# Chunk scores in two matmuls of 128 rows, squares of the FFN's norm summed on VectorE, first weights in quarters

## Chip, cores and metric

The kernel runs on one core of one Trainium2 chip. The metric is the time of one execution on the device in microseconds; the median of three runs is given, and one further execution was profiled. Data are in float32; TensorE multiplies in fp32r, so each operand is held as a high half and the rest.

## The reference

Two layers, each an attention block with three groups of heads and a gated FFN with a causal convolution, for 512 positions of width 1024. The part that the change touches:

```python
def chunk_attention(h, rel_bias):
    q, k, v = [t.reshape(B, nc, CHUNK, CH_HEADS, CH_HD) for t in jnp.split(h, 3, axis=-1)]
    ...
    s = jnp.einsum('bnqhd,bnkhd->bnhqk', q, kb).astype(jnp.float32) * (CH_HD ** -0.5)
    ...
    p = jax.nn.softmax(s, axis=-1)
...
for l in range(DEPTH):
    proj = rms_norm(x, attn_norm[l]) @ w_in[l]
    h_mla, h_diff, h_ch = jnp.split(proj, [IN_MLA, IN_MLA + IN_DIFF], axis=-1)
    ...
    x = x + jnp.concatenate([o_mla, o_diff, o_ch], axis=-1) @ w_out[l]
    x = x + conv_ffn(rms_norm(x, ffn_norm[l]), w_ffn_in[l], ffn_conv_w[l], ffn_conv_b[l], w_ffn_out[l])
```

There are 4 chunk heads of 64 dimensions, 6 MLA heads and 6 differential heads. `rms_norm` divides by the root of the mean of squares over the 1024 columns.

## The kernel before

Positions lie along the free axis: x is held transposed as 8 tiles of 128 x 512 in `xa`, and a product (`proj`) takes 128 columns of weights in 24 matmuls of 512 columns: for 8 tiles of x, high weights with the high and the rest of x, then the rest of the weights with the high of x. Weights arrive by SP into one of two raw slots (`wraw`), are split into `wh` and `wl`, and pass through rings of three. PSUM has three banks for products (psproj), two for scores (pss), two for transposes and norms (pspt), one for values (psav).

The jobs of a layer stand in a queue (`ORDER`): kv, q0, q1 and so on for the latent part, d0 to d2 (query and key of two differential heads each), c0 and c1 (query and key of two chunk heads each), values, then the output projection a0 to a7 (inputs that are ready early) and b0, b1 (the last two inputs, four tiles of x each). A job starts when its gate opens. Beside the queue two streams run: `scores`, which takes the heads in the order m, d, c (`HEADS`), two heads of each name, four row blocks each, and `products`, which turns and multiplies the probabilities. A planner (`Clock`) keeps a model of costs, lets the first ready step go to PE, and at the end lists all instructions of all engines in a new order by a critical path (`list_schedule`). All instructions are issued from there, so the profile shows nearly all of them under one line, L364, and groups are told apart by tiles: `af` holds float32 scratch, `ar` the split operands and probabilities.

- A chunk score (`chunk_head`, `three`) multiplies 64 rows: high with high, high with rest, rest with high, three matmuls a row block. The two heads of a tile use rows 0 to 63 and 64 to 127. A differential score has its operands stacked to 96 rows by copies on POOL's queue (`stack`), an MLA score has 128 rows.
- The FFN's norm (`Gain.add`) splits each tile of x after the output projection has been added to it (`add_to_x`, VectorE): ScalarE makes the high half, VectorE the rest, ScalarE the square, and POOL adds the square to the sum (`gain_f.add(..., pool)` in `run_b`). `add_to_x` also frees the product's bank.
- At the start `load_inputs` issues x tile by tile, with the first product's weights in two halves before and after the first tile, the second product's (also two halves) behind the second tile; the third product's follow when a raw slot is free. PE also sums the squares of x itself (`Gain.squares`, pspt from `af` and `ones`).

Of the kernel before, what the change touches and what calls it, by code (L numbers as in the profile page):

```python
# [20 lines left out]
S = 512  # L21
# [31 lines left out]
for u in range(2):  # L53
    RINGS_R[f"cq{u}"], RINGS_R[f"ck{u}"] = ([RINGS_R["kmla"][2 * u + n]] for n in range(2))
    RINGS_R[f"vc{u}"] = [v[1 + u]]
# [8 lines left out]
p0, o0, ol0 = (RINGS_F[t][1] for t in ("P", "o", "ol"))  # L64
RINGS_F["oc"], RINGS_F["om"], RINGS_F["od"] = (S, o0[0:2]), (S, o0[0:3]), (S, o0[3:6])
# [15 lines left out]
ORDER = "kv q0 q1 kr e0 v e1 u0 u1 u2 d0 d1 d2 e2 c0 c1 g0 g1 a0 a1 a2 a3 a4 a5 a6 a7 b0 b1"  # L81
# [8 lines left out]
AHEAD = 1  # L90
NB_OUT = 1 << (8 // KB).bit_length() - 1
# [388 lines left out]
def encoder(ctx, tc, xT, pos_row, pos_col, wflat, small, lam, relx, cst, out):  # L480
# [17 lines left out]
    def T(tag):  # L498
        turn[tag] = turn.get(tag, -1) + 1
        if tag in RINGS_R:  # L500
            n = RINGS_R[tag][turn[tag] % len(RINGS_R[tag])]
            return ar[:, n * 1024 : (n + 1) * 1024]
        w, starts = RINGS_F[tag]
        o = starts[turn[tag] % len(starts)]
        return af[:, o : o + w]
# [33 lines left out]
    def weights(l, name, run, finish, gate=lambda: True):  # L539
        o, c = offs[l, name]  # L540
        runs = [(0, c // 2), (c // 2, c)] if l == 0 and len(work.jobs) < 3 else [(0, c)]
# [4 lines left out]
        def fetch():  # L546
            raw = T("wraw")
            part(raw, *runs[0])
            if work.jobs[0].raw is None:
                rest_of_first.append(lambda: part(raw, *runs[1]))  # L550
            elif len(runs) > 1:
                part(raw, *runs[1])
            return raw
# [35 lines left out]


# [19 lines left out]
    def load_inputs():  # L610

        work.jobs[0].fetch()
        sp.dma_start(sm[0], small[0])
        for k in range(KD):
            sp.dma_start(xs[k], xT[:, k, :])
            if k == 0:
                rest_of_first.pop()()
            if k == 1:
                work.jobs[1].fetch()
        sp.dma_start(posk_i, bass.AP(tensor=pos_row.tensor, offset=0, ap=[[0, P], [1, S]]))  # L620
        sp.dma_start(ct, cst)
        sp.dma_start(posq_i, pos_col)
# [260 lines left out]
    def layer(l, gain_a):  # L883
# [52 lines left out]
        def chunk_qk(u):  # L936
            gate = lambda: (1, 1, 1) in stacks if u else ("m", 2, 1) in scored
            return [qk_unit(f"cq_{u}", f"cq{u}", gate, imm=CH_SCALE), qk_unit(f"ck_{u}", f"ck{u}", gate)]
# [130 lines left out]
        def chunk_head(h, qt, kt, buf, res):  # L1069
            rbias = biases[h]  # L1070
            yield from softmax_rows(three(qt, kt, 64 * (h % 2), 64), lambda i: rbias[:, S - 128 * (i + 1) :], -1.0, res, buf)
            scaled(*res)
            if h + 2 < CH_H:
                biases.append(load_bias(h + 2))
# [69 lines left out]
        def run_b(t, w):  # L1144
            for n in range(NB_OUT):
                c = slice(128 * KB * n, 128 * KB * (n + 1))
                acc = yield from proj(og[KA:], (w[0][:, c], w[1][:, c]), [])
                add_to_x(NB_OUT * t + n, acc)
                gain_f.add(NB_OUT * t + n, pool)

        jobs = {}

        def job(name):
            kind, t = name[0], int(name[1:]) if name[1:].isdigit() else 0
            return {
                "c": lambda: chunk_qk(t),
# [94 lines left out]
        if l == 0:  # L1251
            load_inputs()
            exp_tables()
            work.jobs[0].load()
            for k in range(KD):
                gain_a.split(k)
                if k in (1, 4):
                    work.jobs[1 + k // 4].load()
            gain_a.squares()
            setup_rope()  # L1260
# [9 lines left out]
        def scores():  # L1270
            for n, (kind, u, j) in enumerate(heads):

                over = max((k + 1 for k in range(n) if bufs[k] in bufs[n] + "X" * (kind == "d")), default=0)
                need = [jobs[f"u{u}"]] if kind == "m" else jobs[f"{kind}{u}"][:2]
# [252 lines left out]
```

## Time and profile before

| what | value |
|---|---|
| median of three runs | 1240.6 us (1240.38 to 1242.81) |
| the profiled execution | 1241.23 us, its span 1239.1 us |
| PE busy | 1215.1 us, 5607 matmuls |
| VectorE (DVE), ScalarE (ACT), POOL busy | 861.0, 704.2, 123.0 us |
| mean granted clock of TensorE | 0.995 |

An engine's busy time is the union of its instructions. A matmul's row shows its start and its duration with the latency of the pipeline, so rows of PE overlap; the cost of one in a stream is read from ends. In brackets behind a row stands the idle time before it, with what ended it.

### The profile page before, as it was taken

What the parts mean: (1) busy time and instruction counts of PE and PEld (TensorE: products, weight loads), DVE (VectorE), ACT (ScalarE), POOL (GpSimd) and SP (SyncE); (2) the same over time, 40 slices, a digit from 0 to 9 for tenths busy, and PEclk for the clock granted to TensorE, in tenths of its full rate; (3) what the DMA queues carried; (4) which work ended last, traced back from release to release, by engine and by line L of the source; (5) the groups of instructions that cost most, each with busy time, mean ns of one, the idle gap of its engine ahead of it and who ended that gap; (6) DMA issues with size and microseconds to landing.
All of it is one profiled execution on the core that took longest, in us unless ns stands there. A gap on an engine that the chain in (4) does not pass through costs nothing.

```text
span 1239.1 us, 15626 instructions
## 1 busy us (share of the span) xinstructions
PE 1215.1 (98%) x5607; PEld 991.1 (80%) x5607; DVE 861.0 (69%) x1596; ACT 704.2 (57%) x1233; POOL 123.0 (10%) x181
## 2 busy tenths in 40 slices
PE   8999999999999999999999999999999999999996
PEld 5788887788888888888877888777888888888885
DVE  7798997588774357665457889976876633677643
ACT  6797996765443234444477899876544422444432
POOL 0214310130000000000011143003100000000000
PEclk9999999999999999999999999999999999999998
DMA  5848961733322332323477498436333233332232
GB/s 169 188 104 186 227 134 43 166 103 122 102 87 82 104 105 100 102 81 91 127 163 163 100 235 175 93 79 151 103 102 102 77 97 116 102 96 91 79 97 79
DMA packets 51613, 146.33 MB, mean 118 GB/s; under 512 B 6480, under 2 KB 9552, under 8 KB 51536
## 3 DMA queue, kind: packets, MB, share of 16 engines
q1 hardware_dynamic: 37280, 106.27, 28.1%
q0 software_dynamic: 14256, 39.07, 17.5%
q8 instruction: 44, 0.72, 0.2%
q14 instruction: 33, 0.27, 0.1%
HBM read 132.21 MB, written 2.10 MB: 108 GB/s over the span
## 4 chain that ended last, share of the span: by engine, by line
PE 92%; DVE 3%; ACT 2%; DMA 2%; issue 1%; SPq 0%; DVEq 0%; ACTq 0%; POOLq 0%
PE psproj L364 80%; PE pss L364 5%; PE pspt L364 4%; PE psav L364 3%; DVE af L364 1%; DVE ar L364 1%; DMA ar<-in_wflat 1%; ACT ar L364 1%; ACT af L364 1%; DVE xa L364 1%; DMA xa<-in_xT 1%; DMA af<-in_wflat 0%; SPq L364 0%; ACT L880 0%; ACT rope L364 0%
## 5 line engine op out<-in xcount | busy, mean ns | idle before, releaser
L364 PE MATMUL psproj<-ar 128*128 128x512 f32 (+1 forms) x4595 | 1104.7, 392 | 8.3 <-DVE xa L364 2.2
L364 PEld LDWEIGHTS psproj<-ar 128*128 128x128 f32 x4595 | 849.3, 188 | 184.7 <-DVE ar L364 4.7
L364 ACT CAST ar<-af 128x512 fp32r<-128x512 f32 (+4 forms) x333 | 268.4, 820 | 219.8 <-PE psproj L364 195.7
L364 DVE TENSOR_TENSOR ar<-af,ar 128x512 fp32r<-128x512 f32 (+4 forms) x260 | 239.7, 925 | 145.3 <-PE psproj L364 79.3
L364 DVE SCALAR_TENSOR_TENSOR af<-af,sma 128x511 f32<-128x511 f32 (+1 forms) x192 | 141.9, 748 | 7.5 <-ACT af L364 4.9
L364 ACT ACTIVATE af<-af,sma 128x512 f32<-128x512 f32 x88 | 71.3, 816 | 121.2 <-DVE af L364 121.2
L364 DVE TENSOR_TENSOR af<-psproj,af 128x512 f32<-128x512 f32 x108 | 73.6, 686 | 61.4 <-PE psproj L364 61.0
L364 POOL DMA_DIRECT2D ar<-in_wflat x61 | 54.0, 886 | 617.8 <-ACT ar L364 601.0
L364 ACT ACTIVATE af<-af 128x512 f32<-128x512 f32 (+1 forms) x106 | 65.4, 622 | 71.6 <-DVE af L364 71.0
L364 ACT ACTIVATE af<-af,mn 128x128 f32<-128x128 f32 (+3 forms) x176 | 98.2, 559 | 7.4 <-DVE mn L364 7.0
L364 PE MATMUL pss<-ar 128*128 128x128 f32 (+7 forms) x336 | 88.1, 333 | 0.6 <-DVE mn L364 0.4
L364 PEld LDWEIGHTS pss<-ar 128*128 128x128 f32 (+2 forms) x336 | 56.6, 187 | 19.4 <-issue 7.7
L364 DVE TENSOR_TENSOR xa<-xa,psproj 128x512 f32<-128x512 f32 (+1 forms) x65 | 43.5, 674 | 40.4 <-PE psproj L364 40.3
L364 DVE TENSOR_TENSOR af<-af 128x512 f32<-128x512 f32 (+2 forms) x71 | 48.0, 677 | 33.4 <-ACT af L364 33.0
L364 DVE TENSOR_TENSOR ar<-pspt,ar 128x512 fp32r<-128x512 f32 (+1 forms) x106 | 63.2, 603 | 6.3 <-ACT ar L364 3.5
L364 PE MATMUL psav<-ar 128*128 128x512 f32 (+3 forms) x256 | 64.9, 331 | 0.3 <-DVE af L364 0.2
L364 PE MATMUL pspt<-ident,af 128*128 128x128 f32 x360 | 63.3, 275 | 0.3 <-DVE af L364 0.3
L364 ACT ACTIVATE ar<-af 128x1024 fp32r<-128x1024 f32 (+3 forms) x61 | 58.0, 950 | 8.0 <-PE psproj L364 5.6
L364 PEld LDWEIGHTS pspt<-ident,af 128*128 128x128 f32 x360 | 45.2, 140 | 14.4 <-DVE af L364 2.3
L364 PEld LDWEIGHTS psav<-ar 128*128 128x128 f32 x256 | 44.6, 189 | 8.8 <-issue 1.3
L364 ACT CAST ar<-pspt 128x512 fp32r<-128x512 f32 (+1 forms) x73 | 37.6, 524 | 17.1 <-PE pspt L364 15.5
L364 DVE CUSTOM_DVE_ANT_0 af<-pss,dist 128x384 f32<-128x384 f32 (+2 forms) x96 | 45.3, 484 | 2.9 <-PE pss L364 2.8
(67 smaller groups left out, 564.2 us busy)
## 6 DMA issues: line engine op xcount, KB each, us to landing
af<-in_wflat SPq DMA_DIRECT2D x125, 512.0 KB, 3.5
ar<-in_wflat POOLq DMA_DIRECT2D x37, 512.0 KB, 8.0
af<-in_wflat SPq DMA_DIRECT2D x48, 384.0 KB, 3.0
af<-in_wflat SPq DMA_DIRECT2D x38, 320.0 KB, 2.9
ar<-ar POOLq DMA_DIRECT2D x72, 128.0 KB, 6.2
ar<-in_wflat POOLq DMA_DIRECT2D x16, 384.0 KB, 6.2
xa<-in_xT SPq DMA_DIRECT2D x8, 256.0 KB, 6.8
af<-in_wflat SPq DMA_DIRECT2D x8, 256.0 KB, 3.8
```

Source lines behind the costliest of these rows:

```text
L364: self.clock.issue(self.name, op, outs, ins + aps, func, lambda: fn(*args, **kw))
```

## The change

Chunk scores: `chunk_qk` becomes `chunk_q` and `chunk_k`. A query tile now holds, for each of its two heads, the high half in the head's own 64 rows and the rest in the other 64. A key tile for each head holds high and rest in its own rows, and a copy on POOL's queue puts the same into the other 64 rows. Two matmuls of 128 rows then sum all four products. The keys of the second head of each pair need another slot (`cy`, the first two slots of ring x, which the stacks of the last differential heads read from), so the gate of both key jobs is the last stack of the differential heads. The key jobs have their own names, y0 and y1, in the queue: c0 y0 c1 y1.

FFN's norm: `gain_f.add` is called without POOL, so the squares are summed on VectorE.

Start: the first three products' weights come in four quarters each, one of each product with every second tile of x, and the third product has a raw slot of its own (`wfirst`).

```diff
...
+    RINGS_R[f"cy{u}"] = [RINGS_R["x"][u]]
...
+RINGS_F["wfirst"] = (2 * S, o0[0:1])
...
-ORDER = "kv q0 q1 kr e0 v e1 u0 u1 u2 d0 d1 d2 e2 c0 c1 g0 g1 a0 a1 a2 a3 a4 a5 a6 a7 b0 b1"
+ORDER = "kv q0 q1 kr e0 v e1 u0 u1 u2 d0 d1 d2 e2 c0 y0 c1 y1 g0 g1 a0 a1 a2 a3 a4 a5 a6 a7 b0 b1"
...
+FIRST = 4
...
-        runs = [(0, c // 2), (c // 2, c)] if l == 0 and len(work.jobs) < 3 else [(0, c)]
+        first = l == 0 and len(work.jobs) < 3
+        step = c // FIRST if first else c
+        runs = [(a, a + step) for a in range(0, c, step)]
+        ring = "wfirst" if first and len(work.jobs) == 2 else "wraw"
-            raw = T("wraw")
-            part(raw, *runs[0])
-            if work.jobs[0].raw is None:
-                rest_of_first.append(lambda: part(raw, *runs[1]))
-            elif len(runs) > 1:
-                part(raw, *runs[1])
+            raw = T(ring)
+            if first:
+                rest_of_first.append([lambda a=a, b=b: part(raw, a, b) for a, b in runs])
+            else:
+                part(raw, 0, c)
...
+    def high(src, hi):
+        n = hi.ap[-1][1]
+        if clock.through("act", 0.1 + n / 1200, src) < clock.through("dve", 0.07 + n / 1920, src) + LATE["hs"]:
+            act.copy(hi, src)
+        else:
+            dve.tensor_copy(hi, src)
...
-        work.jobs[0].fetch()
+        for n in range(3):
+            work.jobs[n].fetch()
-            if k == 0:
-                rest_of_first.pop()()
-            if k == 1:
-                work.jobs[1].fetch()
+            if k % (KD // FIRST) == 0:
+                for parts in rest_of_first:
+                    parts.pop(0)()
...
-        def chunk_qk(u):
-            gate = lambda: (1, 1, 1) in stacks if u else ("m", 2, 1) in scored
-            return [qk_unit(f"cq_{u}", f"cq{u}", gate, imm=CH_SCALE), qk_unit(f"ck_{u}", f"ck{u}", gate)]
+        def chunk_q(u):
+            def finish(job, acc, rb):
+                f = tmp("ev")
+                dve.scalar_tensor_tensor(f, acc, CH_SCALE, rb, op0=ALU.mult, op1=ALU.mult)
+                t = pair(f"cq{u}")
+                for j in range(2):
+                    own, other = slice(64 * j, 64 * j + 64), slice(64 - 64 * j, 128 - 64 * j)
+                    high(f[own, :], t[own, j, :])
+                    dve.tensor_tensor(t[other, j, :], f[own, :], t[own, j, :].bitcast(F32), op=ALU.subtract)
+                job.set(t)
+            return unit(f"cq_{u}", gain_a, finish, lambda: (1, 1, 1) in stacks if u else ("m", 2, 1) in scored)
+        def chunk_k(u):
+            def finish(job, acc, rb):
+                f = tmp("ev")
+                dve.tensor_tensor(f, acc, rb, op=ALU.mult)
+                ks = [pair(f"ck{u}"), pair(f"cy{u}")]
+                for j, t in enumerate(ks):
+                    own, other = slice(64 * j, 64 * j + 64), slice(64 - 64 * j, 128 - 64 * j)
+                    high(f[own, :], t[own, 0, :])
+                    dve.tensor_tensor(t[own, 1, :], f[own, :], t[own, 0, :].bitcast(F32), op=ALU.subtract)
+                    pool.dma_start(t[other, :, :], t[own, :, :])
+                job.set(ks)
+            return unit(f"ck_{u}", gain_a, finish, lambda: (2, 1, 1) in stacks)
...
-            yield from softmax_rows(three(qt, kt, 64 * (h % 2), 64), lambda i: rbias[:, S - 128 * (i + 1) :], -1.0, res, buf)
+            yield from softmax_rows([(qt[:, h % 2, :], kt[h % 2][:, n, :]) for n in range(2)], lambda i: rbias[:, S - 128 * (i + 1) :], -1.0, res, buf)
...
-                gain_f.add(NB_OUT * t + n, pool)
+                gain_f.add(NB_OUT * t + n)
-                "c": lambda: chunk_qk(t),
+                "c": lambda: chunk_q(t),
+                "y": lambda: chunk_k(t),
...
-            work.jobs[0].load()
+            for n in range(3):
+                work.jobs[n].load()
-                if k in (1, 4):
-                    work.jobs[1 + k // 4].load()
...
-                need = [jobs[f"u{u}"]] if kind == "m" else jobs[f"{kind}{u}"][:2]
+                need = [jobs[f"u{u}"]] if kind == "m" else jobs[f"d{u}"][:2] if kind == "d" else [jobs[f"c{u}"], jobs[f"y{u}"]]
...
```

What the planner makes of it, in three places. On PE, in layer 0's chunk heads, before (pss are scores, psproj products, psav values, pspt transposes; 128 is what a score writes, the rows that it reads are not printed):

```order
L364 MATMUL psproj_63<-ar 128x512 x4
L364 MATMUL psproj_65<-ar 128x512
L364 MATMUL psproj_63<-ar 128x512
L364 MATMUL pss_67<-ar 128x512 x3
L364 MATMUL psav_70<-ar 128x512
L364 MATMUL psproj_63<-ar 128x512
L364 MATMUL psproj_65<-ar 128x512
L364 MATMUL pspt_69<-ident,af 128x128 x2
L364 MATMUL psproj_65<-ar 128x512
```

and now, at the first chunk head of layer 0:

```order
L368 MATMUL psproj_63<-ar 128x512
L368 MATMUL pss_67<-ar 128x256 x2
L368 MATMUL psproj_63<-ar 128x512
L368 MATMUL psproj_65<-ar 128x512 x2
L368 MATMUL psproj_63<-ar 128x512 x3
L368 MATMUL psav_70<-ar 128x512
L368 MATMUL pss_66<-ar 128x384 x2
L368 MATMUL psproj_64<-ar 128x512
L368 MATMUL pspt_69<-ident,af 128x128 x2
```

A row block's scores were three and are two; what stands between them is of the same kinds.

On VectorE, in the norm of layer 1's FFN, before (xa are additions to x, which free a product's bank; SCALAR_TENSOR_TENSOR from xa are the splits):

```order
L364 TENSOR_TENSOR xa<-xa,psproj_63 128x512
L364 SCALAR_TENSOR_TENSOR ar<-xa,sma,ar 128x512
L364 TENSOR_TENSOR xa<-xa,psproj_64 128x512
L364 SCALAR_TENSOR_TENSOR ar<-xa,sma,ar 128x512 x3
L364 TENSOR_TENSOR xa<-xa,psproj_65 128x512
L364 TENSOR_TENSOR xa<-xa,psproj_63 128x512
L364 TENSOR_TENSOR xa<-xa,psproj_64 128x512
L364 SCALAR_TENSOR_TENSOR ar<-xa,sma,ar 128x512
L364 TENSOR_TENSOR xa<-xa,psproj_65 128x512
```

and now (TENSOR_TENSOR af<-af 128x512 is the sum of squares):

```order
L368 TENSOR_TENSOR xa<-xa,psproj_64 128x512
L368 SCALAR_TENSOR_TENSOR ar<-xa,sma,ar 128x512
L368 TENSOR_TENSOR af<-af 128x512
L368 SCALAR_TENSOR_TENSOR ar<-xa,sma,ar 128x512
L368 TENSOR_TENSOR xa<-xa,psproj_65 128x512
L368 TENSOR_TENSOR af<-af 128x512
L368 SCALAR_TENSOR_TENSOR ar<-xa,sma,ar 128x512
L368 TENSOR_TENSOR xa<-xa,psproj_63 128x512
L368 TENSOR_TENSOR af<-af 128x512
L368 TENSOR_TENSOR xa<-xa,psproj_64 128x512
```

Between the additions from psproj_64 and psproj_65 three splits became a split, a sum and a split, and two or three operations now stand between the later additions.

On PE at the start, before (pspt from af and ones are the squares of one tile of x; psproj_63, 64, 65 are the first three products):

```order
L364 MATMUL pspt_68<-eps,ones 128x512
L364 MATMUL pspt_68<-af,ones 128x512
L364 MATMUL psproj_63<-ar 128x512 x3
L364 MATMUL pspt_68<-af,ones 128x512
L364 MATMUL psproj_63<-ar 128x512
L364 MATMUL psproj_64<-ar 128x512 x3
L364 MATMUL psproj_63<-ar 128x512
L364 MATMUL psproj_64<-ar 128x512 x2
```

and now:

```order
L368 MATMUL pspt_68<-eps,ones 128x512
L368 MATMUL pspt_68<-af,ones 128x512
L368 MATMUL psproj_63<-ar 128x512
L368 MATMUL psproj_64<-ar 128x512
L368 MATMUL psproj_63<-ar 128x512
L368 MATMUL psproj_64<-ar 128x512
L368 MATMUL psproj_63<-ar 128x512
L368 MATMUL psproj_65<-ar 128x512
L368 MATMUL pspt_68<-af,ones 128x512
```

Ahead of the second tile's squares six matmuls of three products replace three of one.

## Rows read from the trace of the kernel before

**Rows 1.** The page, busy us (share of the span) and instructions of an engine.
```profile
...
PE 1215.1 (98%) x5607; PEld 991.1 (80%) x5607; DVE 861.0 (69%) x1596; ACT 704.2 (57%) x1233; POOL 123.0 (10%) x181
...
```

**Rows 2.** What PE waited for: us in total, times, longest us.
```profile
...
PE psproj L364 <- DVE xa L364: 2.2, 1, 2.2
...
```

**Rows 3.** Timeline of PE, 128-row scores: start us, us, operation.
```profile
...
60.67 1.31 PE L364 MATMUL psproj<-ar 128*128 128x512 f32 x5
61.83 0.86 PE L364 MATMUL pss<-ar 128*128 128x512 f32 x3
62.52 1.07 PE L364 MATMUL psproj<-ar 128*128 128x512 f32 x4
...
```

**Rows 4.** Timeline of PE, chunk heads of layer 0, and layer 1's last run.
```profile
...
183.78 0.55 PE L364 MATMUL pss<-ar 64*128 64x128 f32 x3
...
187.38 0.79 PE L364 MATMUL pss<-ar 64*128 64x384 f32 x3
...
189.61 0.50 PE L364 MATMUL pss<-ar 64*128 64x512 f32 x1
...
193.12 0.32 PE L364 MATMUL pss<-ar 64*128 64x128 f32 x1
...
198.54 0.44 PE L364 MATMUL pss<-ar 64*128 64x384 f32 x1
...
200.17 1.62 PE L364 MATMUL psproj<-ar 128*128 128x512 f32 x6
201.72 0.96 PE L364 MATMUL pss<-ar 64*128 64x512 f32 x3
202.61 0.50 PE L364 MATMUL psav<-ar 128*128 128x512 f32 x1
...
823.57 0.96 PE L364 MATMUL pss<-ar 64*128 64x512 f32 x3
...
```

**Rows 5.** Windows: us, then PE, PEld, DVE, ACT, POOL busy; clock, DMA share, GB/s.
```profile
...
160.00:183.00 23.00, 23.00 (x120) 19.10 (x119) 22.60 (x66) 22.41 (x53) 3.36 (x5) 1.00 0.68 150
...
183.00:222.00 39.00, 39.00 (x186) 27.23 (x185) 31.43 (x89) 27.54 (x66) 2.02 (x4) 1.00 0.24 55
787.00:826.00 39.00, 39.00 (x191) 27.59 (x190) 32.18 (x87) 27.50 (x67) 3.15 (x5) 1.00 0.39 82
...
```

**Rows 6.** Timeline of VectorE (DVE) near the start.
```profile
...
22.57 0.68 DVE L364 TENSOR_TENSOR ar<-af,ar 128x512 fp32r<-128x512 f32 x1
23.17 0.69 DVE L364 SCALAR_TENSOR_TENSOR af<-af 128x512 f32<-128x512 f32 x1
...
```

**Rows 7.** Timeline of all engines, norm of layer 1's FFN.
```profile
...
857.58 5.03 POOL L364 TENSOR_TENSOR af<-af 128x512 f32<-128x512 f32 x3 [6.46 <-ACT af L364]
857.99 0.68 DVE L364 TENSOR_TENSOR xa<-xa,psproj 128x512 f32<-128x512 f32 x1
...
858.59 4.57 DVE L364 SCALAR_TENSOR_TENSOR ar<-xa,sma,ar 128x512 fp32r<-128x512 f32 x3
...
863.08 1.87 DVE L364 TENSOR_TENSOR xa<-xa,psproj 128x512 f32<-128x512 f32 x3
...
863.81 10.08 PE L364 MATMUL psproj<-ar 128*128 128x512 f32 x43 [2.21 <-DVE xa L364]
864.88 0.74 DVE L364 SCALAR_TENSOR_TENSOR ar<-xa,sma,ar 128x512 fp32r<-128x512 f32 x1
...
```

**Rows 8.** Timeline of PE at the start.
```profile
...
9.12 0.80 PE L364 MATMUL psproj<-ar 128*128 128x512 f32 x1 [1.68 <-ACT ar L364]
...
9.71 2.00 PE L364 MATMUL pspt<-af,ones 128*128 128x512 f32 x2
...
13.69 1.02 PE L364 MATMUL pspt<-af,ones 128*128 128x512 f32 x2
...
```

**Rows 9.** Timeline of VectorE, a subtraction of 64 rows.
```profile
...
43.83 0.69 DVE L364 TENSOR_TENSOR ar<-af,ar 64x512 fp32r<-64x512 f32 x1
...
```

**Rows 10.** DMA issues in 0 to 50: count, KB each, median us to landing.
```profile
...
ar<-ar POOLq DMA_DIRECT2D x3, 256.0 KB, 9.7
...
```

## The prediction

> **What bounds the kernel now.** I read the page's busy shares first. TensorE's matmuls are busy for 1215.1 of the span's 1239.1 us [rows 1], so the kernel is one long PE stream, and an edit pays only if it takes work out of that stream or closes a hole in it. The holes come next, in the table of what PE waited for: the longest entry is one single wait of 2.2 us, on an addition to x by VectorE [rows 2]. The end is no place to look: nothing of the change is in the last tile. What a busy share hides is seen only in PE's timeline, by adding start and duration of a row to get its modelled end and comparing ends. Undisturbed, three scores of 128 rows and 512 columns, which follow matmuls that end at 60.67 + 1.31 = 61.98, end at 62.69, 0.71 later, and the four products behind them take 0.90, or 0.225 each [rows 3]. The chunk scores have 64 rows. Three of them follow matmuls that end at 201.79 and end at 202.68, 0.89 later; the one matmul behind them ends at 203.11, 0.43 later [rows 4]. So going into 64 rows costs 0.18 us more than staying in 128 rows, and coming back 0.20: PE counts as busy, and 0.38 us is lost at every run of 64-row scores.
>
> **Part 1, chunk scores.** For each of 4 heads in 2 layers and 4 row blocks, three 64-row matmuls become two of 128 rows: the query tile carries its high half in one half of the rows and its rest in the other, and the key tile carries the same values twice. 32 matmuls go. One matmul more in a run costs the spacing inside it, a run of three less a run of one, halved: (0.96 - 0.50)/2 = 0.23 for 512 columns, (0.79 - 0.44)/2 = 0.175 for 384, (0.55 - 0.32)/2 = 0.115 for 128 [rows 4], and for 256 between the last two, some 0.12. That is 0.64 a head, 5.1 us for eight. The runs of 64 rows are 21 in layer 0, the first at 183.78, and 19 in layer 1, the last at 823.57 [rows 4]; 40 x 0.38 = 15.2 us. All of this lies on PE, which waits for nothing in these stretches, so the sum on PE is 20.3 us.
>
> At this place a rule speaks against the row. The Trainium skill (TensorE: Matmul & The Clock Gate, Why this matters for your kernels) says that a matmul of few rows takes as long as one of 128 and that its gain is to run beside others in other row groups. By it the change would give the 5.1 us alone, and would give up that concurrency; the rows above show 0.89 against 0.71, so I go by them.
>
> What this part adds: each q and k product is now split in two halves of 64 rows, and a 64-row subtraction on VectorE takes 0.69 us, no less than a full one [rows 9]. Eight products get one copy (ScalarE or VectorE) and one subtraction more: 8 x 0.69 = 5.5 us of VectorE. The windows show what room there is. In 183 to 222 us PE has 39.0, VectorE 31.43 busy; in 787 to 826 VectorE has 32.18 [rows 5]. PE's need falls to 39.0 - 21 x 0.38 - 4 x 0.64 = 28.5 and 39.0 - 19 x 0.38 - 2.6 = 29.2. If 31.43 and 32.18 were hard needs, VectorE would hand back 2.9 + 3.0 = 5.9 us, and up to 5.5 more. They are not quite: back to back, operations that last 0.68 start 0.60 apart [rows 6], and in the diff heads just before VectorE runs at 22.60 of 23.00 [rows 5] without holding PE. 31.43 x 0.60/0.69 + 2.8 = 30.1 against 28.5 gives back 1.6, in layer 1 30.8 against 29.2 gives 1.6, and part of the 2.8 falls into the diff heads. Between 0 and 11.4 I take 2.0, near the squeezed reading, since the full diff stretch shows the squeeze.
>
> The keys are copied to the other 64 rows by eight new transfers of 256 KB on POOL's queue. The nearest row is 9.7 us from issue to landing for 256 KB [rows 10]. The gate of both key products is now the last stack of the diff heads, and the two d2 heads stand between it and the first chunk score; these two fill the window of 23 us ahead of the first chunk score at 183.78 [rows 4, 5], so this is hidden. But VectorE's second key half waits for the stack's transfers to have read the x slot, and the scores of d2 are queued behind it on VectorE. Bounds 0 and one such landing tail a layer, some 2 us each; I take 1.0 in all.
>
> **Part 2, the sums of squares on VectorE.** While POOL adds squares, VectorE's three splits take 4.57 us, against 0.74 for the one at 864.88, because both engines crawl: POOL's three additions take 5.03 [rows 7]. Behind these three splits stands the addition that frees PE's bank (863.08), and PE waits 2.21 us (863.81), all in [rows 7]. With POOL's additions gone, the order puts a split, an addition of squares and a split there: 3 x 0.65 after the addition of 857.99 instead of 4.57, so that bank comes some 2.5 us earlier. The next bank, though, now has two more VectorE operations ahead of it: each tile costs VectorE an addition to x, a split and a sum, about 0.65 each and so 2.0 us, where PE needs 6 matmuls of 0.225, 1.35 us. I leave 0.7 of the wait: gain 1.5, bounds 0 (the wait only moves on to the next bank) and 2.2. In layer 0 nothing is to be had: the wait is one occasion, not two [rows 2].
>
> **Part 3, the first weights in quarters.** Ahead of the last tile of x the queue now carries five quarters (640 KB) instead of three halves (768 KB), so x lands hardly earlier, and with two issues more on SP. PE's hole before the second tile of x is 1.68 us [rows 8]; two products stand ahead of it and the third, at 9.12, behind it, where the new order has six ahead of the second norm matmul: four more, at most 4 x 0.225 = 0.9 us. The early pair of norm matmuls takes 2.00, the one at 13.69 takes 1.02 [rows 8]: early matmuls run at half the later rate, though the profile's granted clock shows no lower level there. If a fuller start ends that earlier, at most half of the 4.0 us from 9.71 to 13.69 comes back, 2.0. Against it: twelve more operations on VectorE in a stretch where it works back to back [rows 6]. Bounds 2.9 gained and, at 0.08 for each of the twelve (0.68 less 0.60), 1.0 lost; I take 0.7 gained, most of the filled hole, since that is the part that the rows show.
>
> **Sum.** 5.1 + 15.2 + 1.5 + 0.7 - 2.0 - 1.0 = 19.5 us from the profiled execution's 1241.2 gives 1221.7; the median of the three runs lies 0.6 under that execution, so 1221.
>
> **Rivals.** (A) VectorE becomes the bound of the chunk heads: 5.9 us handed back, and half of the added 5.5, 8.6 instead of 2.0: 1227 to 1228. For it: 31.43 and 32.18 of 39 and full neighbours; against: the squeeze. (B) The 0.38 us belongs to something else than the row count (the change of bank, of operand), and stays: 1241.2 - 5.1 - 1.5 - 0.7 + 1.0 = 1234.9, so 1234. The skill's rule above would end here. Against it: the scores of 128 rows change banks and operands too, and show 0.71. (C) Slower than before: the key copies land too late and PE, with its fill used up, stands at the first score of a chunk head. Four heads' first copies a run exposed in full, two a layer, are 4 x 9.7 = 38.8 against a gain of 22.5: 1257. It decides from 22.5/9.7 = 2.3 copies on. For it: the later gate; against: two diff heads between. The Trainium skill (SBUF — State Buffer, Who interferes with whom) adds that a transfer issued by POOL waits for its descriptors while VectorE copies in its fast mode; no row here shows that apart, and it only helps this rival.
>
> **How the numbers follow.** Forecast 0.72, A 0.15, B 0.08, C 0.05. Low end: all terms at their best, 5.1 + 15.2 + 2.2 + 2.9 = 25.4, so 1241.2 - 25.4 - 0.6 = 1215.2, or 1215. High end: it reaches to A, 1228, and leaves out B and C and little of A. A measurement of this kernel tells some 0.2%, 2.5 us, from no change; all cases but C are faster by more, and a half-exposed C is the same or slower: faster 0.94, same 0.02, slower 0.04.
>
> **What would show it.** Right: no 64-row scores, 64 in 128 rows; the end of a matmul behind scores comes 0.23 after the last; a chunk pair shrinks by some 9 us a layer; POOL has no additions, VectorE's splits take 0.75 and PE's wait near 863 is under 1 us; the first products end about 1 us earlier. Wrong: PE waits on VectorE between the chunk scores (A), 0.38 us remains around the scores (B), or PE waits on a transfer of ar from ar (C). All of it falls if PE's stream turns out to hold new holes in the diff heads.

## The result and the profile after

| | before | after |
|---|---|---|
| median | 1241.34 us (1240.38 to 1242.81, 4 runs) | 1224.55 us (1222.39 to 1225.84, 4 runs) |
| ratio | | 0.9862, interval 0.9844 to 0.9880 |
| profiled execution, its span | 1241.23, 1239.1 us | 1224.15, 1222.4 us |

The change makes the kernel 16.8 us faster by the medians; forecast were 19.5 and 1221 us. The time lies inside the range, but nearer to rival A's 1227 (2.5 us away) than to the forecast (3.6), and the range took in both. PE's busy time fell with the span, so PE is still the engine that sets it (page after: busy us, share, instructions; answers to [rows 1]):

```profile
PE 1199.9 (98%) x5575; PEld 986.1 (81%) x5575; DVE 860.8 (70%) x1628; ACT 708.5 (58%) x1243; POOL 104.6 (9%) x175
```

**The row switch is gone.** Timeline of PE after, around a chunk score of layer 0 (start us, us, operation), to be held against [rows 4]:

```profile
...
199.57 0.28 PE L368 MATMUL psav<-ar 128*128 128x256 f32 x1
199.69 0.40 PE L368 MATMUL pss<-ar 128*128 128x512 f32 x1
199.93 0.40 PE L368 MATMUL psproj<-ar 128*128 128x512 f32 x1
...
```

The ends are 199.85, 200.09 and 200.33: 0.24 into the score and 0.24 out of it, where [rows 4] had 0.89 for three and 0.43 behind them. Over all chunk heads, by the same ends, the 96 scores of 64 rows took 22.6 us of PE before, and the matmuls behind their 40 runs 7.3 us more than such matmuls take elsewhere; the 64 scores of 128 rows take 10.3. That is 19.7 us of PE, where the prediction had 20.3.

**VectorE is full there now.** The windows from the first score of the first chunk head to the first score of the fourth, two rows of before, then two of after (us, then PE, PEld, DVE, ACT and POOL busy with instructions; clock, DMA share, GB/s):

```profile
183.78:212.66 28.88, 28.88 (x140) 20.41 (x139) 23.31 (x68) 19.82 (x49) 1.15 (x3) 1.00 0.20 48
787.41:817.62 30.21, 30.21 (x148) 21.44 (x147) 24.91 (x68) 21.20 (x50) 2.30 (x4) 1.00 0.38 82
```

```profile
178.34:200.95 22.61, 22.61 (x131) 19.03 (x129) 22.52 (x67) 20.70 (x50) 3.69 (x8) 1.00 0.53 120
779.22:801.97 22.75, 22.75 (x133) 19.53 (x132) 21.51 (x63) 20.85 (x51) 2.61 (x5) 1.00 0.54 123
```

Three heads take 6.27 and 7.46 us less. In layer 0 VectorE is now busy for 22.52 of 22.61 us, and PE still has no hole. The holes come behind it. The same columns for the 12 us that follow the fourth head's first score, before and after:

```profile
212.66:224.66 12.00, 12.00 (x58) 8.71 (x58) 9.92 (x28) 9.60 (x22) 1.39 (x2) 1.00 0.32 66
817.62:829.62 12.00, 12.00 (x61) 9.03 (x61) 10.34 (x28) 9.50 (x22) 1.73 (x2) 1.00 0.35 71
```

```profile
200.95:212.95 12.00, 9.73 (x52) 7.13 (x50) 11.81 (x29) 10.76 (x26) 1.74 (x2) 1.00 0.31 68
801.97:813.97 12.00, 10.60 (x59) 8.23 (x57) 11.90 (x33) 11.52 (x25) 1.73 (x2) 1.00 0.42 91
```

PE stands for 2.27 and 1.40 us, while VectorE works 11.81 and 11.90 of 12. Two of the waits in PE's timeline after:

```profile
...
204.24 0.39 PE L368 MATMUL pss<-ar 128*128 128x256 f32 x1 [0.83 <-DVE mn L368]
...
211.33 0.44 PE L368 MATMUL pspt<-ident,af 128*128 128x128 f32 x2 [0.44 <-DVE ar L368]
...
```

The first is a score that waits until VectorE has emptied a bank, the second a transpose that waits for VectorE's split.

**Where the 16.7 us of span came from**, by the starts of the first score of each head (both kernels have the same 502 products ahead of the first chunk score; forecast split here: three of four heads, and half of what was handed back for each layer):

| stretch | before us | after us | difference | forecast |
|---|---|---|---|---|
| start to first chunk score, layer 0 | 183.78 | 178.34 | -5.4 | -0.7 |
| three chunk heads | 28.88 | 22.61 | -6.3 | -7.9 |
| fourth head to first score of layer 1 | 451.19 | 453.42 | +2.2 | -1.1 |
| to first chunk score, layer 1 | 123.56 | 124.85 | +1.3 | 0 |
| three chunk heads | 30.21 | 22.75 | -7.5 | -7.3 |
| fourth head to the end | 421.5 | 420.4 | -1.1 | -2.4 |

The sum was near, but its parts were not: the start came out 4.7 us better than forecast, the stretches from the first chunk head on 7.4 us worse, most of it behind the chunk heads.

### The profile page after: what moved, and what is told of

Read it like the earlier page. It is cut to its first block, busy times and chain, and to the rows that moved or that the text cites. A ratio compares the mean times of both kernels' runs of the same rounds, so it can differ in the third digit from the quotient of the medians.

```text
span 1222.4 us, 15622 instructions
## 1 busy us (share of the span) xinstructions
PE 1199.9 (98%) x5575; PEld 986.1 (81%) x5575; DVE 860.8 (70%) x1628; ACT 708.5 (58%) x1243; POOL 104.6 (9%) x175
## 4 chain that ended last, share of the span: by engine, by line
PE 73%; DVE 3%; issue 1%; DMA 1%; ACT 1%; POOL 0%; DVEq 0%; POOLq 0%; ACTq 0%
PE psproj L368 69%; DVE af L368 2%; PE pss L368 2%; PE pspt L368 1%; DMA ar<-in_wflat 1%; PE psav L368 1%; DVE ar L368 1%; ACT af L368 1%; DVE xa L368 0%; ACT ar L368 0%; POOL ar L368 0%; DVEq L1559 0%; DVE mn L368 0%; ACT xa L368 0%; DVE rl L368 0%
## 5 line engine op out<-in xcount | busy, mean ns | idle before, releaser
L368 ACT CAST ar<-af 128x1024 fp32r<-128x1024 f32 (+4 forms) x341 | 272.7, 815 | 218.6 <-PE psproj L368 197.7
L368 DVE TENSOR_TENSOR ar<-af,ar 128x512 fp32r<-128x512 f32 (+5 forms) x274 | 244.1, 893 | 149.2 <-PE psproj L368 79.6
L368 ACT ACTIVATE af<-af,mn 128x512 f32<-128x512 f32 (+3 forms) x176 | 98.0, 558 | 4.3 <-DVE mn L368 3.7
L368 DVE TENSOR_TENSOR af<-af 128x512 f32<-128x512 f32 (+2 forms) x85 | 57.6, 678 | 34.5 <-ACT af L368 34.1
L368 PE MATMUL pss<-ar 128*128 128x256 f32 (+7 forms) x304 | 80.4, 328 | 1.3 <-DVE mn L368 1.0
L368 PEld LDWEIGHTS pss<-ar 128*128 128x128 f32 (+1 forms) x304 | 53.3, 189 | 12.5 <-DVE mn L368 4.5
L368 PEld LDWEIGHTS pspt<-ident,af 128*128 128x128 f32 x360 | 45.6, 140 | 14.9 <-DVE af L368 2.1
L368 POOL DMA_DIRECT2D ar<-ar x86 | 47.2, 574 | 74.6 <-PE pss L368 16.0
```

The source lines that it names most:

```text
L368: self.clock.issue(self.name, op, outs, ins + aps, func, lambda: fn(*args, **kw))
```

## The experiments

Each kernel is given by its ratio to the kernel before on the same chip, since medians of the kernel before differ by 1.7 us between chips. 0.001 is 1.24 us.

### The three parts, alone and in pairs

The chunk scores alone: the changed kernel with the two other parts taken back, in short

```diff
...
-                gain_f.add(NB_OUT * t + n)
+                gain_f.add(NB_OUT * t + n, pool)
...
-            for n in range(3):
-                work.jobs[n].load()
+            work.jobs[0].load()
...
```

> The kernel before with the chunk scores in two matmuls of 128 rows alone (new query and key tiles, copies on POOL's queue, later gate); the squares of the FFN's norm stay on POOL, the first weights come as before. Theory 1 (the sum of the prediction): 20.3 us off PE less 3.0 handed back, so 17.3 us faster than before, 1223 to 1225. Theory 2 (from the trace of the changed kernel, where TensorE's work of the chunk heads fell by as much as forecast, but new waits for VectorE stand between 200 and 217 us and between 804 and 819): 5 to 9 us of the 20.3 are handed back and only 11 to 14 us are left, 1227 to 1230. Theory 1 is out if the time is above 1226.

Measured: 1231.41 us, ratio 0.9931 (0.9917 to 0.9945), so 8.6 us. Theory 1 is out, and theory 2 was too high as well. The waits list has an entry of 4.5 us in four waits on the addition to x, and the timeline shows what [rows 7] showed in layer 1, now in layer 0 too:

```profile
...
247.96 5.03 POOL L365 TENSOR_TENSOR af<-af 128x512 f32<-128x512 f32 x3 [6.87 <-ACT af L365]
...
248.97 4.57 DVE L365 SCALAR_TENSOR_TENSOR ar<-xa,sma,ar 128x512 fp32r<-128x512 f32 x3
...
254.19 2.12 PE L365 MATMUL psproj<-ar 128*128 128x512 f32 x8 [2.21 <-DVE xa L365]
...
```

So the new order of the chunk part alone opens a stall that part 2 removes.

The squares alone:

```diff
-                gain_f.add(NB_OUT * t + n, pool)
+                gain_f.add(NB_OUT * t + n)
```

> The kernel before with the squares of the FFN's norm summed on VectorE alone. Theory 1 (the prediction): 1.5 us faster, all of it at layer 1's FFN norm, 1239 to 1240. Theory 2 (the trace of the changed kernel, where the wait of 2.2 us shrank to 0.4): some 2 us. Rival: nothing, since the changed kernel's short wait there is owed to another order that the other two parts gave. The trace decides: PE's wait on the addition to x near 863 us is under 1 us by the first two, over 1.5 by the rival.

Measured: 1237.52 us, ratio 0.9984 (0.9974 to 0.9994), 2.0 us. PE's wait on the addition to x is down to 0.2 us in its trace, so the rival is out; theories 1 and 2 can't be told apart by it.

The first weights alone:

```diff
...
-        runs = [(0, c // 2), (c // 2, c)] if l == 0 and len(work.jobs) < 3 else [(0, c)]
+        first = l == 0 and len(work.jobs) < 3
+        step = c // FIRST if first else c
+        runs = [(a, a + step) for a in range(0, c, step)]
+        ring = "wfirst" if first and len(work.jobs) == 2 else "wraw"
...
```

> The kernel before with the first three products' weights in quarters and the third raw slot alone. Theory 1 (the prediction): 0.7 us faster, within -1.0 and +2.9, 1240.5. Theory 2 (the trace of the changed kernel, whose first score of layer 0 starts 3.1 us earlier and its first differential score 5.1 earlier): 4 to 5 us faster, 1236 to 1237, and the waits of PE between 43 and 47 us and at 59.8 are gone. If those 5 us were owed to the later order of the chunk jobs instead, this kernel gains 3 us at most.

Measured: 1244.48 us (1236.94 to 1248.49), ratio 1.0029 (1.0006 to 1.0052): slower, which no theory had. The gain at the start is there: the 241st matmul starts at 63.22 us, against 67.71 before. It is lost where the granted clock falls (the profiled execution is the slowest of its runs). Windows of the kernel before, then of this one:

```profile
200.00:208.00 8.00, 8.00 (x39) 5.74 (x37) 6.36 (x18) 7.32 (x19) 0.15 (x1) 1.00 0.10 35
208.00:222.00 14.00, 14.00 (x68) 9.62 (x67) 11.47 (x29) 9.76 (x22) 0.87 (x1) 1.00 0.24 51
```

```profile
200.00:208.00 8.00, 7.59 (x36) 5.06 (x34) 6.50 (x20) 6.08 (x16) 0.19 (x1) 1.00 0.13 35
208.00:222.00 14.00, 14.00 (x43) 9.64 (x42) 9.62 (x25) 9.14 (x23) 0.86 (x1) 0.51 0.13 32
```

At 0.51, the lower of the two levels, 43 matmuls start in 14 us instead of 68, and PE counts as busy all the time. Ahead of the fall, which the trace records at 208.20, stands one wait of 0.41 us that ended at 207.31. Its runs at a mean granted clock of 0.997 take 1237 us, the one at 0.986 takes 1248.5.

The chunk scores back, the other two parts kept: the kernel above with `gain_f.add` without POOL.

> The kernel before with the squares on VectorE and the first weights in quarters, the chunk scores in three matmuls of 64 rows. Adding up: 2.5 us (squares alone) and 4.5 us (what TensorE loses less in the first 75 us in every kernel with the quarters) faster than before, 1233, ratio 0.994 to 0.995. Rival (the half clock that the kernel with the quarters alone shows from 208 to 221 us comes with its order of work, in which the chunk heads have few products left to stand between the 64-row scores): it is back in some runs, the runs spread by 10 us with their mean granted clock, and the median lies between 1236 and 1244, ratio 0.998 to 1.003.

Measured: 1240.88 us, ratio 1.0005 (0.9994 to 1.0017); the rival holds, the sum of parts does not. Its runs spread by 7 us, at mean granted clocks of 0.988 to 0.994. The same window:

```profile
208.00:222.00 14.00, 14.00 (x48) 9.74 (x48) 10.30 (x26) 10.08 (x25) 0.86 (x1) 0.63 0.19 45
```

The squares back on POOL in the changed kernel (the one line above, reversed):

> The changed kernel with the squares of the FFN's norm added by POOL again. Theory 1 (the prediction): it loses 1.5 to 2 us, all in layer 1, 1226 to 1227. Theory 2 (the part depends on the others: in the kernel with the chunk part alone the stall of 2.2 us on an addition to x stands in both layers): it loses 4 to 5 us, 1228.5 to 1229.5, and PE waits over 2 us for an addition to x near 245 and near 865 us.

Measured: 1227.89 us, ratio 0.9898 (0.9881 to 0.9915), 4.5 us worse than the changed kernel's 0.9862 (3.3 by the medians), with some 3 us of uncertainty. That is theory 2's size. But the profiled execution is one of the two fastest of the five (1225.21 us, with a span only 1.0 us longer than the changed kernel's), and in it the two waits are 0.81 us (at 248.35) and 1.55 (at 848.57), not over 2. So theory 2's mechanism is shown in part only, and what the slower runs lose is open.

The first weights back in the changed kernel:

> The changed kernel with the first weights as before (halves, third product's behind them, no third raw slot). Theory 1 (the prediction): it loses 0.7 us, 1225.3. Theory 2 (the five us that the trace shows before 60 us are this part's own): it loses 4 to 6 us, 1228.5 to 1230.5. Rival (this part costs 4 us with it as it does alone): it is faster than the changed kernel, 1221 or less, and then shows a higher mean granted clock.

Measured: 1228.94 us, ratio 0.9912 (0.9899 to 0.9926), 6.2 us worse (4.4 by the medians). Theory 2 holds, theory 1 and the rival are out. All eight combinations now stand (ratio to before):

| | weights as before | weights in quarters |
|---|---|---|
| neither | 1 | 1.0029 |
| squares on VectorE | 0.9984 | 1.0005 |
| chunk scores | 0.9931 | 0.9898 |
| both | 0.9912 | 0.9862 |

The quarters cost 0.002 to 0.003 beside 64-row scores and gain 0.003 to 0.005 beside 128-row ones. The chunk part is worth 8.6 us alone and 17.7 us on top of the other two.

### What the rows and the third matmul cost

Two of three 64-row matmuls in the kernel before:

```diff
-            yield from softmax_rows(three(qt, kt, 64 * (h % 2), 64), lambda i: rbias[:, S - 128 * (i + 1) :], -1.0, res, buf)
+            yield from softmax_rows(three(qt, kt, 64 * (h % 2), 64)[:2], lambda i: rbias[:, S - 128 * (i + 1) :], -1.0, res, buf)
```

> The kernel before with two of the three 64-row matmuls of each chunk score (the query's rest is left out, so the scores are slightly less exact). Theory 1 (the switch between 64 and 128 rows is paid for each run, and a matmul less is worth 0.16 us, 5.1 in all, since PE waits for nothing there): 5 us faster than before, 1235, and the end of the first matmul behind scores still comes 0.43 after the last. Rival B (the 15 us belong to the count of matmuls): 1220 to 1225. Third case (a third matmul is hidden here too, as in the changed kernel with three matmuls of 128 rows): within 1.5 us of before.

Measured: 1234.95 us, ratio 0.9960 (0.9947 to 0.9973), 5.0 us: theory 1's number, and rival B is out. That it agrees to the tenth is partly chance. The profiled span is 6.4 us shorter than before, and 4.2 of these are gained by the 241st matmul (63.50 against 67.71), far ahead of any chunk score and with the weights as before. What bears the price out is PE's own account: by the ends, its 64 scores take 17.1 us where the kernel before has 22.6 for 96. Its timeline still has the switch:

```profile
...
207.80 0.50 PE L364 MATMUL psproj<-ar 128*128 128x512 f32 x1
208.23 0.38 PE L364 MATMUL pss<-ar 64*128 64x256 f32 x1
208.54 0.50 PE L364 MATMUL psproj<-ar 128*128 128x512 f32 x1
...
```

The ends are 208.30, 208.61 and 209.04: a single 64-row matmul of 256 columns takes 0.31, and the one behind it 0.43.

A third 128-row matmul in the changed kernel:

```diff
-            yield from softmax_rows([(qt[:, h % 2, :], kt[h % 2][:, n, :]) for n in range(2)], lambda i: rbias[:, S - 128 * (i + 1) :], -1.0, res, buf)
+            yield from softmax_rows([(qt[:, h % 2, :], kt[h % 2][:, n, :]) for n in (0, 1, 1)], lambda i: rbias[:, S - 128 * (i + 1) :], -1.0, res, buf)
```

> The changed kernel with a third 128-row matmul in each row block's score (the keys' rest is multiplied twice, so the output is another one). It has 5607 matmuls as before, but none of 64 rows. Theory 1 (what is paid before is the switch between 64 and 128 rows, 15.2 us, and 5.1 for the third matmul): it loses the 5.1 us again, less what falls into waits for VectorE, 1226 to 1230, and still lies 10 us or more under before; a matmul behind scores ends 0.23 after the last. Rival B (the extra 0.38 us belongs to the count of matmuls in a run, or to the change of bank): the time goes back to 1238 or more.

Measured: 1225.23 us, ratio 0.9885 (0.9868 to 0.9903): with as many matmuls as before, 1.15% under before, so the count isn't what gains. Against the changed kernel it is 0.7 us worse by the medians, 2.9 by the ratios, so less than the 5.1 us that the third matmul costs in the kernel before. The scores themselves take 4.6 us more of PE (14.9 by the ends, against 10.3); the rest of that is made good elsewhere in PE's stream, where its other matmuls then wait less.

### What hands the time back

Fewer operations for the halves:

```diff
-                for j in range(2):
-                    own, other = slice(64 * j, 64 * j + 64), slice(64 - 64 * j, 128 - 64 * j)
-                    high(f[own, :], t[own, j, :])
-                    dve.tensor_tensor(t[other, j, :], f[own, :], t[own, j, :].bitcast(F32), op=ALU.subtract)
+                high(f, t[:, 0, :])
+                dve.tensor_tensor(t[:, 1, :], f, t[:, 0, :].bitcast(F32), op=ALU.subtract)
...
```

> The changed kernel without the operations that the half splits add: query and key are split in one copy and one subtraction over all 128 rows and the copies on POOL's queue are taken from there, so the scores are sums of other products. 8 subtractions (5.5 us of VectorE) and 8 copies less; matmuls, their rows and the number of POOL's transfers are the same. Theory 2 (VectorE's added work is what hands back what TensorE gained in the chunk heads): 3 to 5 us faster, 1220 to 1222, with less waiting of PE between 200 and 217 us and 804 and 819. Rival (the chunk heads are held by the chain of the diff heads' norm and of the probabilities, which this doesn't shorten): within 1 us of the changed kernel.

Measured: 1220.47 us, ratio 0.9841 (0.9821 to 0.9862): 2.6 us better than the changed kernel by the ratios, 4.1 by the medians, with intervals that overlap. Behind the fourth head's first score PE stands for 0.41 and 0.36 us of 12, not 2.27 and 1.40:

```profile
201.73:213.73 12.00, 11.59 (x68) 9.21 (x66) 11.73 (x33) 10.90 (x23) 1.73 (x2) 1.00 0.48 106
795.49:807.49 12.00, 11.64 (x64) 9.26 (x63) 11.94 (x30) 10.32 (x24) 1.72 (x2) 1.00 0.24 50
```

The keys split once, with the same result:

```diff
-                for j, t in enumerate(ks):
-                    own, other = slice(64 * j, 64 * j + 64), slice(64 - 64 * j, 128 - 64 * j)
-                    high(f[own, :], t[own, 0, :])
-                    dve.tensor_tensor(t[own, 1, :], f[own, :], t[own, 0, :].bitcast(F32), op=ALU.subtract)
-                    pool.dma_start(t[other, :, :], t[own, :, :])
+                high(f, ks[0][:, 0, :])
+                dve.tensor_tensor(ks[0][:, 1, :], f, ks[0][:, 0, :].bitcast(F32), op=ALU.subtract)
+                for to, at in ((ks[1][64:128, :, :], ks[0][64:128, :, :]), (ks[1][0:64, :, :], ks[0][64:128, :, :]), (ks[0][64:128, :, :], ks[0][0:64, :, :])):
+                    pool.dma_start(to, at)
```

> The changed kernel with the chunk keys split in one copy and one subtraction over all 128 rows, and three copies a pair on POOL's queue in the place of two, the third behind the first two; the result is the same. Four subtractions of 64 rows and four copies less, 2.8 us each of VectorE and ScalarE. Theory 2 (VectorE's load in the chunk heads): 1 to 2 us faster than the changed kernel, ratio 0.9845 to 0.9855. Rival C of the prediction, in small (the copies land too late, now two landings of 6 us in a row): PE waits for a transfer of ar from ar before a chunk head's first score, and it is 3 us or more slower, ratio over 0.9885.

Measured: 1220.34 us (1219.61 to 1220.91), ratio 0.9837 (0.9822 to 0.9853): the best of all kernels, ahead of the changed one by 3.1 us by the ratios, whose intervals overlap a little, and by 4.2 by the medians, more than theory 2's 1 to 2; each of its runs lies under each of the changed kernel's, on another chip. PE never waits for a transfer of ar from ar, although two landings stand in a row: rival C is out with room to spare.

No scaling of the rows:

```diff
-            scaled(*res)
             if h + 2 < CH_H:
```

> The changed kernel without the division of the chunk heads' probabilities by their sums (four scalings a head, on VectorE or ScalarE, some 1.7 us, 14 us in all; the output is unscaled). Theory 2 (VectorE and ScalarE are the bound of the chunk heads since PE got shorter): the waits of PE between 200 and 217 us and between 801 and 819 fall by half or more, 4 to 6 us faster than the changed kernel, ratio to before 0.981 to 0.983. Rival (a chain of latencies, the norm of the last diff heads, holds PE there): the waits stay, ratio 0.985 to 0.987.

Measured: 1227.27 us, ratio 0.9888 (0.9871 to 0.9905): 3.2 us worse, where theory 2 had 4 to 6 better. The windows (three heads of layer 0, then 12 us behind) show why one half of it holds:

```profile
180.55:199.61 19.06, 19.06 (x110) 16.34 (x110) 19.00 (x55) 16.23 (x42) 2.02 (x6) 1.00 0.47 112
199.61:211.61 12.00, 11.79 (x70) 9.70 (x70) 11.55 (x28) 10.27 (x26) 0.16 (x1) 1.00 0.01 2
```

VectorE has 3.5 us less to do (19.00 for 22.52), the three heads are 3.5 us shorter, and the hole behind them is gone. But PE issues only 110 matmuls in them instead of 131, the rest is left for later, and a few us on it waits for weights, after which the clock falls:

```profile
...
218.65 0.73 PE L368 MATMUL psproj<-ar 128*128 128x512 f32 x2 [1.66 <-DMA ar<-in_wflat]
```

```profile
216.00:224.00 8.00, 6.34 (x19) 4.72 (x20) 2.07 (x3) 3.45 (x7) 0.85 (x1) 0.79 0.86 201
```

A dearer VectorE in the planner:

```diff
-            cost = 0.069 + 0.061 * ptr + n / (1920 if fast else 960)
+            cost = 0.085 + 0.061 * ptr + n / (1920 if fast else 960)
```

> The changed kernel with the planner's fixed cost of a VectorE operation raised from 0.069 to 0.085 us, so that its order holds VectorE for slower; nothing else. Theory 2 (load): the same work has to be done, within 2 us of the changed kernel, ratio 0.985 to 0.988. Rival (the order is at fault: PE stands at a score whose bank is late while other matmuls could run): the waits in the chunk heads fall, 3 us or more faster, ratio under 0.984.

Measured: 1235.27 us, ratio 0.9960 (0.9946 to 0.9975), 12 us worse; neither theory. The work is the same, only its order differs, and the three heads of layer 0 have holes of 2 us and a fallen clock:

```profile
180.12:206.17 26.05, 24.09 (x122) 19.69 (x120) 24.76 (x67) 20.03 (x49) 2.85 (x7) 0.87 0.32 74
```

So VectorE's load makes the holes behind the chunk heads (two kernels with less of it have almost none, 0.41 and 0.36 us with fewer halves, 0.55 and 0.23 with the keys split once, and are faster), but the time of this stretch hangs as much on what the planner leaves for PE to do there. How the time handed back divides between the two stays open.

## Why the prediction was right, step by step

- **What bounds the kernel.** Right: PE is busy for 98% before and after, and what was gained was work taken out of its stream and holes closed. The waits list before has a second single wait of 2.2 us beside the one named (on ar by VectorE, near 651 us); the change leaves it, 1.81 after.
- **The switch, 15.2 us.** Right. It is gone in the changed kernel (0.24 and 0.24 instead of 0.89 and 0.43), and it stays with two 64-row matmuls. There the time into a run and out of it, above that of staying in 128 rows, sums to 14.4 us over 38 runs, 0.18 on the way in and 0.19 on the way out; in the kernel before it is 14.7 over 40. The Trainium skill (TensorEngine Tiling (Array Packing), Key Properties) says that a change of tiling mode drains TensorE; the trace agrees in so far as each change between 64 and 128 rows costs time, and gives the price; that it is a drain, no run here shows apart. The Trainium skill's rule on few rows, weighed in the prediction, holds inside a run (0.23 us for 512 columns with 64 rows as with 128), but did not decide: rival B would have ended near 1234.
- **The third matmul, 5.1 us.** Right as a price on PE (with two 64-row matmuls, 17.1 us for 64 scores against 22.6 for 96), though the 5.0 us by which that kernel's median is lower don't prove it; too much as a gain here: put back, it cost 0.7 to 2.9 us.
- **What VectorE gives back, 2.0.** Too small, and in the wrong place. I looked for it inside the chunk heads, where PE fills up with products and has no hole though VectorE is full (22.52 of 22.61). It stands behind them: holes of 2.27 and 1.40 us in the 12 us after the fourth head's first score. These are 3.7 of the 7.4 us by which the stretches from the chunk heads on missed the forecast. The prediction's own sign for rival A, PE waiting on VectorE at a chunk score, is there, at the fourth head (204.24). The rest shows little as idle time: outside the windows the longest wait behind layer 0's chunk heads is 0.57, at 231.31, but for two near 640 (1.13 and 1.81) that have their like before (0.75 and 2.20). Some 5 us lie in matmuls that end later than their form usually does without a hole in front of them, 1.5 to 1.8 us more than before in each of the three stretches behind the chunk heads of the table above. What holds them was not followed up. With the 3.0 that I had put down, some 10 us were handed back, somewhat more than rival A's price (8.6). That the time came out between the forecast and A's 1227, and not at A's or above, is luck: it is owed to the start.
- **The key copies, 1.0.** No matmul waits for a transfer of ar from ar in any kernel, even with two landings in a row (in the kernel with the chunk scores alone one weight load does, for 0.2 us). Layer 1 lost 1.3 us ahead of the chunk heads; whether the second key half's wait is in it was not told apart.
- **The squares, 1.5.** Right in kind: the waits list after has this entry in the place of [rows 2], 2.2 us:

```profile
PE psproj L368 <- DVE xa L368: 0.7, 2, 0.3
```

  So 1.5 there, 2.0 measured alone, 4.5 in the whole kernel. That layer 0 has nothing to give was true of the order before only; the chunk part alone opens the same 2.21 there. The additions and splits that stood side by side ([rows 7]) took 5.03 and 4.57 in layer 0 of that kernel, 5.08 and 4.15 in layer 1, and each split takes 0.74 after (start 843.82):

```profile
843.82 0.74 DVE L368 SCALAR_TENSOR_TENSOR ar<-xa,sma,ar 128x512 fp32r<-128x512 f32 x1
844.48 0.68 DVE L368 TENSOR_TENSOR af<-af 128x512 f32<-128x512 f32 x1
```

- **The quarters, 0.7.** The step that failed. I took only the hole at 9.12 ([rows 8]), bounded the rest by 2.9 and closed the account at 14 us. Three things came together. The hole went from 1.68 to 0.21 us:

```profile
8.46 1.22 PE L368 MATMUL psproj<-ar 128*128 128x512 f32 x2 [0.21 <-ACT ar L368]
```

  PE's slow early matmuls end sooner. The prediction read that the granted clock shows no lower level there. But the trace's first record of the clock is at 12.72 us (at 10.06 after), and the views print 1.00 where there is none. Ahead of that record products of 512 columns end 0.43 us apart, behind it 0.23, in both traces, and 0.43 is their spacing in the stretch at 0.51 above too: PE begins at its lower level. Seven products ahead of the record in the kernel with the first weights back (its record is at 14.96), and seven behind it in the one with two 64-row matmuls (7.56):

```profile
10.94 3.98 PE L365 MATMUL psproj<-ar 128*128 128x512 f32 x7
```

```profile
8.95 2.17 PE L364 MATMUL psproj<-ar 128*128 128x512 f32 x7
```

  A record 2.7 us earlier is worth some 1.2 us (an estimate from the two spacings); with the hole, the 41st matmul starts at 19.50 us, against 21.63. And PE no longer waits between 43 and 60 us, 2.0 us in the kernel before, which my sum never looked at. The longest of these waits has no row after, and its entry stood in the waits list before:

```profile
59.81 0.50 PE L364 MATMUL psproj<-ar 128*128 128x512 f32 x1 [1.37 <-DMA ar<-in_wflat]
```

```profile
PE psproj L364 <- DMA ar<-in_wflat: 2.1, 2, 1.4
```

  The 241st matmul starts at 61.7 to 63.2 us in the nine kernels with the quarters (62.5 on average), at 63.5 to 68.8 in the five without (67.0): 4.5 us, and 4.5 to 6.2 in the four pairs that differ in the quarters alone. How much of it is the quarters' own stays open. The 63.5 is reached without them, with the early record at 7.56. And the kernel with the squares back, whose PE begins with the same matmuls as the changed kernel's, has its record at 7.77, not 10.06, and starts the 241st 0.9 us earlier: the order of PE's work alone does not set it.
- **The sum** came out within 3 us because two errors stand against each other: 4.7 us too little at the start, 7.4 too much from the chunk heads on. And the terms don't add: alone the parts give 8.6, 2.0 and -3.6, which is 7, and together 17. Most of the -3.6 is the fallen clock of the kernel with the quarters alone: its two runs at a mean clock of 0.997 gain 3 us, and with these the sum would be some 14. The prediction had no step for that.

## What to carry to other kernels

Add a matmul's modelled ends, not its busy time, wherever its row count changes; a switch to fewer rows and back can cost more than the matmul. When work leaves the bounding engine, look for what hands time back behind the stretch, where that engine runs out of other work, not in it. Where one planner orders everything, price a change by its neighbours as well: three parts that gave 7 us in sum (some 14 without the fallen clock) gave 17 together, and a constant of the planner moved 12. And when a kernel's time meets a theory to the tenth, look where in the trace the time was gained before taking it as proof.

## What the runs showed of the hardware

- TensorE's granted clock fell to its lower level at 208.20 us in the kernel with the quarters alone and stayed there until 221.85, while PE counts as busy throughout: 43 matmuls in 14 us at 0.51. The one wait near it, 0.41 us, had ended at 207.31; the changed kernel has a longer one (0.83 at 204.24) and stays at 1.00. In the 14 us before, products took 4.66 us of PE, at the like place of the kernel before, where it stayed at 1.00, 6.88 (windows of the products alone, before and then this kernel). What makes it fall was not told apart.

```profile
195.00:209.00 14.00, 6.88 (x20) 3.56 (x21) 0.00 (x0) 0.00 (x0) 1.00 0.06 20
```

```profile
194.00:208.00 14.00, 4.66 (x13) 2.02 (x12) 0.00 (x0) 0.00 (x0) 1.00 0.14 39
```

- It fell too behind a hole of 1.66 us, the wait for weights without row scaling: 0.79 on average from 216 to 224 us.
- TensorE begins at its lower level: in all fourteen traces products of 512 columns that wait for nothing end 0.43 us apart until the first record of the granted clock, 7.6 to 15.0 us into the span, and 0.23 apart behind it.
- Three splits on VectorE beside three additions on POOL take 4.57 us (the additions 5.03), against 0.74 for a split alone. The Trainium skill (SBUF — State Buffer, SBUF: two separate sides) has an exclusive lock between the two for a VectorE operation with two inputs in SBUF against a POOL operation that reads SBUF; the rows agree.
- A change between 64 and 128 rows costs PE 0.18 us on the way in and 0.18 to 0.19 on the way back; one between 96 and 128 rows under 0.01.
